# Three edits to an encoder trunk on one core: the order of split products, the queue of a DMA, and blank matmuls at the start

## The chip, the cores and the metric

The kernel runs on one core of one Trainium2 chip. The metric is the time of one execution on the device in microseconds (us); lower is better. Engines are named as in the profile: PE is TensorE's matmul side and PEld its weight loads, DVE is VectorE, ACT is ScalarE, POOL is GpSimd, SP is SyncE, which here only issues DMAs.

## What is computed

A two-layer encoder over 256 tokens of width 2048, all in float32. The reference, cut to its frame:

```python
for i in range(DEPTH):                       # DEPTH = 2
    h = rms_norm(x, norm_mix_g[i])
    if i % 2 == 0:                           # retention heads and 2-D neighbourhood attention
        x = x + retention_na_mixer(h, w_in_ab[j], ..., w_out_ab[j])
    else:                                    # differential attention
        x = x + diff_attention_mixer(h, w_in_c[j], ..., w_out_c[j], i)
    m = rms_norm(mem, norm_mem_g[i])
    x = x + memory_cross_attention(rms_norm(x, norm_xattn_g[i]), m, w_xq[i], w_xkv[i], w_xo[i], ...)
    x = x + swiglu_ffn(rms_norm(x, norm_ffn_g[i]), w_ffn_in[i], w_ffn_out[i])
```

Nearly all of the work is in the products of the 256 token rows with the weight matrices, some 453 MB of weights that are each read once.

## The kernel before, in words

Every weight product runs through `gemm` (line 297). A matrix is cut into column blocks of 512, and a block into units of 256 rows of the matrix (two tiles of 128). A load from HBM (`raw`, 1 MB, three buffers, issued by SP at line 282) holds two units. `prepare` (line 269) makes from half of it the two operands of a unit: ACT rounds the weights to float32r (`wh`, line 292), DVE subtracts to get what is left (`wl`, line 293); each has three buffers. The activations are split in the same way into `hi` and `lo` (tiles named `hTh`/`hTl`, `hTfh`/`hTfl`, `aTh`/`aTl` and so on). A unit is 12 matmuls of 128 x 128 by 512 columns: for each of two token tiles t and each of two weight tiles j, hi times `wh` (line 321), hi times `wl` (322), lo times `wh` (323), all added up in one PSUM tile for each t. `prepare` runs up to three units ahead (`LOOK`).

There are 864 units in 24 products (`plan`, from line 235), in a fixed order. Most products finish one block before the next begins; some begin with two or four blocks interleaved, so that the last rows of the activations may come late. When a block's last unit is done, its `epi` takes the two PSUM tiles away (two blocks' tiles exist), and `Side` (line 30) hands out the other work in small steps, one or two for each unit, each due a number of units after the step before. The framework then orders the instructions of each engine by their priority and by when they should be ready; each engine works through its own queue in order.

`regroup` (line 377) turns a block of 256 x 512 values around without TensorE. DVE transposes 32 x 32 squares (line 389), one DMA of 512 KB writes the squares to HBM (`zd`, line 391, issued by SP), and four DMAs of 128 KB read them back in the other grouping (`zz`, line 394, issued by POOL, each waiting for the write's landing). The reads are handed out two units after the write (`LAND`), and their use three units after that (`MOVE`). `feed` (line 409) uses it for the blocks of the next normalised input: ACT writes hi (line 419), DVE lo (line 421). `act_T` uses it for the FFN's hidden blocks. POOL also computes the powers of `rsqrt_mean` (line 334).

At the start, `feed_first` makes the first input from a transposed copy of x that SP loads in eight parts (`xt`), between the weights. The order of the first units (`start`, line 245) interleaves the first two blocks.

Of the kernel before, what the change touches and what calls it, by code (L numbers as in the profile page):

```python
# [10 lines left out]
F32 = mybir.dt.float32  # L11
# [5 lines left out]
P = 128  # L17
D = 2048
T = 256
# [62 lines left out]
def trunk_kernel(  # L82
# [8 lines left out]
    nc = tc.nc  # L91

    def pool(name, bufs, **kw):
        return ctx.enter_context(tc.tile_pool(name=name, bufs=bufs, **kw))

    const = pool("const", 1)
# [13 lines left out]
    ps_acc = pool("ps_acc", 2, space=bass.MemoryType.PSUM)  # L110
    ps_t = pool("ps_t", 2, space=bass.MemoryType.PSUM)
    ps_a = pool("ps_a", 2, space=bass.MemoryType.PSUM)


    x_sb = const.tile([P, 2, D], F32, name="x_sb")
# [129 lines left out]
    start = [(b, 2 * c + u) for c in range(4) for b in range(2) for u in range(2)]  # L245
    start += [(b, u) for b in range(2, len(cols_ab)) for u in range(8)]
    for layer in range(2):
        j = layer // 2
# [10 lines left out]
        for g0, g1 in FFN_GROUPS:  # L259
            n = 2 * (g1 - g0)  # L260
# [8 lines left out]
    def prepare():  # L269

        i, b, u = units[at["unit"]]
        w2, rows, cols, _ = plan[i]
        c, h = u // 2, u % 2
        if (i, b, c) not in raws:
            raw = raws[i, b, c] = rawp.tile([P, 4, NB], F32, name="raw")
            src = w2[rows[c]:rows[c] + 512, cols[b]:cols[b] + NB].rearrange("(k p) n -> p k n", p=P)
            if at["unit"] == 0:
                nc.sync.dma_start(raw[:, 0:2], src[:, 0:2])
                load_xt(1)
                nc.sync.dma_start(raw[:, 2:4], src[:, 2:4])  # L280
            else:
                nc.sync.dma_start(raw, src)
            for what in OPENING.get(at["unit"], ()):
                (load_xt if what >= 0 else load_x)(what if what >= 0 else -1 - what)
        raw = raws[i, b, c]
        if h:
            del raws[i, b, c]
        wh = hip.tile([P, 2, NB], F32R, name="wh")
        wl = lop.tile([P, 2, NB], F32R, name="wl")
        for j in ((0, 1), (1, 2)) if at["unit"] == 0 else ((0, 2),):  # L290
            js, rs = slice(*j), slice(2 * h + j[0], 2 * h + j[1])
            nc.scalar.copy(wh[:, js], raw[:, rs])  # L292
            nc.vector.tensor_sub(wl[:, js], raw[:, rs], wh[:, js])  # L293
        ahead.append((wh, wl))
        at["unit"] += 1

    def gemm(kts, src, epi, gate=None, steps=1, wide=False):
        hi, lo = src
        w2, rows, cols, order = plan[at["phase"]]
        at["phase"] += 1  # L300
        nu = 2 * len(rows)
        accs, left = {}, {}
        for b, u in order:
            side.drain((gate or {}).get(u, ()))
            if b not in accs:
                pools = ((ps_acc, f"acc{t}") for t in range(2))
                if wide and b in (2, 3):
                    pools = ((ps_t, "pt"), (ps_t, "pt")) if b == 2 else ((ps_a, "pa"), (ps_a, "pa"))
                accs[b] = [q.tile([P, NB], F32, tag=tag, name=f"acc{t}") for t, (q, tag) in enumerate(pools)]
                left[b] = nu  # L310
            while len(ahead) <= LOOK and at["unit"] < len(units):
                prepare()
            wh, wl = ahead.popleft()
            acc = accs[b]
            first, left[b] = left[b] == nu, left[b] - 1
            last = left[b] == 0
            for t in range(2):
                ts = slice(t * P, (t + 1) * P)
                for j in range(2):
                    kt = kts[u // 2] + 2 * (u % 2) + j  # L320
                    nc.tensor.matmul(acc[t], lhsT=hi[:, kt, ts], rhs=wh[:, j], start=first and j == 0, stop=False)  # L321
                    nc.tensor.matmul(acc[t], lhsT=hi[:, kt, ts], rhs=wl[:, j], start=False, stop=False)  # L322
                    nc.tensor.matmul(acc[t], lhsT=lo[:, kt, ts], rhs=wh[:, j], start=False, stop=last and j == 1)  # L323
            if last:
                epi(b, acc)
            side.pump(steps)
# [50 lines left out]
    def regroup(srcs, room=""):  # L377


        if room == "m8":  # L380
            both = m8.tile([P, 2, 4 * T], F32, tag="m8", name="zz")
            zt, zT = both[:, 0], both[:, 1]
        elif room:
            zt, zT = (qk.tile([P, 4 * T], F32, tag=room + x, name="zz") for x in "hl")
        else:
            zt, zT = (vp.tile([P, 4 * T], F32, tag="v" + x, name="zz") for x in "hl")
        zt = zt.rearrange("p (j k t b) -> p j k t b", j=4, k=4, t=2)
        for t in range(2):
            nc.vector.transpose(zt[:, :, :, t], srcs[t].rearrange("p (k j a) -> p j k a", j=4, a=32))
        zd = dram.tile([4, 32, 4, T], F32, name="zd")  # L390
        nc.sync.dma_start(zd.rearrange("i a j n -> (i a) (j n)"), zt.rearrange("p j k t b -> p (j k t b)"))
        yield LAND
        for j in range(4):
            nc.gpsimd.dma_start(zT[32 * j:32 * j + 32].rearrange("a (i n) -> a i n", i=4),  # L394
                                zd[:, :, j].rearrange("i a n -> a i n"))
        yield MOVE - LAND
        return zT.rearrange("p (i k t b) -> p i k t b", i=4, k=4, t=2)
# [11 lines left out]
    def feed(dst, b, srcs, gi, layer, ssr, room):  # L409
        for t in range(2):  # L410
            square_sum(ssr[0][:, t, b:b + 1], srcs[t])
        if b == 3:
            finish_rstd(ssr)
        zT = yield from regroup(srcs, room)
        for k in range(4):
            g = gain(gi, layer, 4 * b + k)
            hi, lo = (x[:, 4 * b + k].rearrange("p (t i b) -> p t i b", t=2, i=4) for x in dst)
            src = zT[:, :, k].rearrange("p i t b -> p t i b")
            nc.scalar.activation(hi, src, AF.Copy, scale=g)
            for t in range(2):  # L420
                nc.vector.scalar_tensor_tensor(out=lo[:, t], in0=src[:, t], scalar=g, in1=hi[:, t].bitcast(F32),
                                               op0=ALU.mult, op1=ALU.subtract)
# [190 lines left out]
    def retention_na(j, hT, rstd, oT, gate):  # L613
# [4 lines left out]
        def epi(b, acc):  # L618
# [26 lines left out]
            else:  # L645
# [9 lines left out]
                tails.append(side.add(gate_T(zs, oT, gi * 4, head_gain(c_ret + j)), 2))  # L655

        gemm(KT4, hT, epi, gate=gate)
        side.drain(tails[:1])
        return {6: tails}
# [46 lines left out]
    def diff_attention(j, hT, rstd, oT, gate):  # L706
        groups = [{} for _ in range(4)]

        def epi(i, acc):
            b, part = i // 3, i % 3  # L710
            g = groups[b]
            if part == 0:
                g["q"], g["tq"] = normed_T(acc, rstd, c_dq + j, "qT")
            elif part == 1:
                g["k"], g["tk"] = normed_T(acc, rstd, c_dk + j, "kT")
                g["tasks"] = [side.add(diff_head(g, hh, 2 * b + hh, j, oT), cond=prepared(g)) for hh in range(2)]
            else:
                g["v"] = tokens(acc, rstd)

        gemm(KT4, hT, epi, gate=gate)  # L720
        for b in range(3):
            side.drain(groups[b]["tasks"])
        return {6: groups[3]["tasks"]}
# [35 lines left out]
    for layer in range(2):  # L759
        j = layer // 2  # L760
        A, B = which
        oT = pair(B, "oT")
        if layer % 2 == 0:
            gate = retention_na(j, hT, ssr[1:], oT, gate)
            kts = (8, 12, 0, 4)
        else:
            nc.vector.scalar_tensor_tensor(out=tabs, in0=tdiff, scalar=-1.0, in1=tdiff, op0=ALU.mult, op1=ALU.max)
            gate = diff_attention(j, hT, ssr[1:], oT, gate)
            kts = KT4
# [21 lines left out]
        mtasks = [side.add(mem_block(b)) for b in range(4)]  # L791

        gemm(kts, oT, lambda b, acc: add_x(acc, b), gate=gate)
        side.drain(mtasks)
        hT = pair(B, "hTx")
# [34 lines left out]
        def act_T(aT, zs, kt):  # L830
            zT = yield from regroup(zs)
            for t in range(2):
                split(*(x[:, kt:kt + 4, t * P:(t + 1) * P].rearrange("p k (i b) -> p k i b", i=4) for x in aT),
                      zT[:, :, :, t].rearrange("p i k b -> p k i b"))

        for g0, g1 in FFN_GROUPS:
            aT = pair(A, "aT")
            n = g1 - g0
# [17 lines left out]
            kts = tuple(4 * b for b in range(n))  # L856
            last = g1 == 11
# [53 lines left out]
```

## Time and profile before

| | us |
|---|---|
| three runs | 2475.91, 2476.86, 2476.88 |
| median | 2476.86 |
| the profiled execution | 2475.84 |
| its span, first to last instruction | 2474.1 |
| PE busy in the span | 2456.3 |

The span is 1.7 us shorter than the time of its own execution. Busy times of PE are modelled from starts, so the distance from one matmul's start to the next is the better measure; it is read from the timeline, where each matmul has its start in the first column.

### The profile page before, as it was taken

What the parts mean: (1) busy time and instruction counts of PE and PEld (TensorE: products, weight loads), DVE (VectorE), ACT (ScalarE), POOL (GpSimd) and SP (SyncE); (2) the same over time, 40 slices, a digit from 0 to 9 for tenths busy, and PEclk for the clock granted to TensorE, in tenths of its full rate; (3) what the DMA queues carried; (4) which work ended last, traced back from release to release, by engine and by line L of the source; (5) the groups of instructions that cost most, each with busy time, mean ns of one, the idle gap of its engine ahead of it and who ended that gap; (6) DMA issues with size and microseconds to landing.
All of it is one profiled execution on the core that took longest, in us unless ns stands there. A gap on an engine that the chain in (4) does not pass through costs nothing.

```text
span 2474.1 us, 28641 instructions
## 1 busy us (share of the span) xinstructions
PE 2456.3 (99%) x11184; PEld 2037.1 (82%) x11184; DVE 1475.7 (60%) x1833; ACT 1187.0 (48%) x1538; POOL 138.2 (6%) x215
## 2 busy tenths in 40 slices
PE   8999999999999999999999999999999999999999
PEld 6888888888888888888888888888888888888887
DVE  6775565675655555555567766767655545555554
ACT  6554464564443444444455555655544444443443
POOL 1000001010000000000010000010100000000000
PEclk9999999999999999999999999999999999999999
DMA  8555567656765666566674555675766656665665
GB/s 288 177 169 179 175 226 245 214 192 213 233 216 200 205 212 225 194 198 226 225 241 164 170 170 168 212 249 171 237 222 210 215 188 214 228 206 200 207 217 175
DMA packets 250184, 511.82 MB, mean 207 GB/s; under 512 B 11328, under 2 KB 11968, under 8 KB 250048
## 3 DMA queue, kind: packets, MB, share of 16 engines
q1 hardware_dynamic: 239568, 484.47, 58.5%
q0 software_dynamic: 8320, 23.08, 4.1%
q10 hardware_dynamic: 2160, 2.44, 0.3%
q8 instruction: 87, 1.43, 0.2%
q14 instruction: 49, 0.40, 0.0%
HBM read 486.88 MB, written 23.07 MB: 206 GB/s over the span
## 4 chain that ended last, share of the span: by engine, by line
PE 92%; DMA 3%; DVE 3%; ACT 1%; POOL 1%; issue 0%; ACTq 0%; SPq 0%; POOLq 0%; DVEq 0%
PE acc L322 30%; PE acc L321 30%; PE acc L323 30%; DMA zz<-zd 2%; DVE wl L293 1%; DMA zd<-zz 1%; PE pt L345 1%; ACT wh L292 0%; PE pt L545 0%; PE pa_s L437 0%; PE pa_s L436 0%; DVE x_sb L741 0%; PE pa_s L435 0%; POOL zz L394 0%; PE pa_r L595 0%
## 5 line engine op out<-in xcount | busy, mean ns | idle before, releaser
L293 DVE TENSOR_TENSOR wl<-raw,wh 128x1024 fp32r<-128x1024 f32 (+1 forms) x865 | 1053.7, 1221 | 870.8 <-ACT wh L292 870.4
L292 ACT CAST wh<-raw 128x1024 fp32r<-128x1024 f32 (+1 forms) x865 | 909.1, 1051 | 1158.2 <-PE acc L323 1132.8
L322 PE MATMUL acc<-wl,hTfh 128*128 128x512 f32 x1408 | 547.9, 389 | 0.6 <-DVE wl L293 0.6
L323 PE MATMUL acc<-wh,hTfl 128*128 128x512 f32 x1408 | 547.7, 389 | 0.0
L321 PE MATMUL acc<-wh,hTfh 128*128 128x512 f32 x1408 | 547.7, 389 | 0.0
L321 PE MATMUL acc<-wh,hTh 128*128 128x512 f32 x832 | 332.0, 399 | 9.8 <-ACT wh L292 8.3
L322 PE MATMUL acc<-wl,hTh 128*128 128x512 f32 x832 | 325.7, 391 | 0.9 <-DVE wl L293 0.9
L323 PE MATMUL acc<-wh,hTl 128*128 128x512 f32 x832 | 325.8, 392 | 0.0
L322 PEld LDWEIGHTS acc<-wl,hTfh 128*128 128x128 f32 x1408 | 264.3, 188 | 56.2 <-DVE wl L293 1.4
L323 PEld LDWEIGHTS acc<-wh,hTfl 128*128 128x128 f32 x1408 | 264.3, 188 | 54.9
L321 PEld LDWEIGHTS acc<-wh,hTfh 128*128 128x128 f32 x1408 | 264.3, 188 | 54.9
L322 PE MATMUL acc<-wl,aTh 128*128 128x512 f32 x704 | 274.0, 389 | 0.2 <-DVE wl L293 0.2
L323 PE MATMUL acc<-wh,aTl 128*128 128x512 f32 x704 | 273.9, 389 | 0.0
L321 PE MATMUL acc<-wh,aTh 128*128 128x512 f32 x704 | 273.9, 389 | 0.0
L321 PEld LDWEIGHTS acc<-wh,hTh 128*128 128x128 f32 x832 | 157.2, 189 | 40.0 <-ACT wh L292 8.3
L323 PEld LDWEIGHTS acc<-wh,hTl 128*128 128x128 f32 x832 | 156.7, 188 | 34.0
L322 PEld LDWEIGHTS acc<-wl,hTh 128*128 128x128 f32 x832 | 157.2, 189 | 31.2 <-DVE wl L293 1.8
L394 POOL DMA_DIRECT2D zz<-zd x160 | 87.3, 552 | 1589.9 <-DMA zd<-zz 1410.9
L322 PEld LDWEIGHTS acc<-wl,aTh 128*128 128x128 f32 x704 | 132.1, 188 | 28.2 <-DVE wl L293 0.8
L321 PEld LDWEIGHTS acc<-wh,aTh 128*128 128x128 f32 x704 | 132.1, 188 | 27.5
L323 PEld LDWEIGHTS acc<-wh,aTl 128*128 128x128 f32 x704 | 132.1, 188 | 27.3
L321 PE MATMUL acc<-wh,oTh 128*128 128x512 f32 x256 | 100.2, 392 | 0.0
(189 smaller groups left out, 1940.3 us busy)
## 6 DMA issues: line engine op xcount, KB each, us to landing
raw<-in_w_ffn_in SPq DMA_DIRECT2D x176, 1024.0 KB, 5.1
raw<-in_w_ffn_out SPq DMA_DIRECT2D x88, 1024.0 KB, 5.1
raw<-in_w_in_ab SPq DMA_DIRECT2D x55, 1024.0 KB, 5.2
raw<-in_w_in_c SPq DMA_DIRECT2D x48, 1024.0 KB, 5.2
zd<-zz SPq DMA_DIRECT2D x40, 512.0 KB, 3.8
zz<-zd POOLq DMA_DIRECT2D x160, 128.0 KB, 5.4
raw<-in_w_out_ab SPq DMA_DIRECT2D x16, 1024.0 KB, 5.1
raw<-in_w_xkv SPq DMA_DIRECT2D x16, 1024.0 KB, 5.0
```

What stands on the lines that cost most here:

```text
L292: nc.scalar.copy(wh[:, js], raw[:, rs])
L293: nc.vector.tensor_sub(wl[:, js], raw[:, rs], wh[:, js])
L321: nc.tensor.matmul(acc[t], lhsT=hi[:, kt, ts], rhs=wh[:, j], start=first and j == 0, stop=False)
L322: nc.tensor.matmul(acc[t], lhsT=hi[:, kt, ts], rhs=wl[:, j], start=False, stop=False)
L323: nc.tensor.matmul(acc[t], lhsT=lo[:, kt, ts], rhs=wh[:, j], start=False, stop=last and j == 1)
L345: nc.tensor.transpose(pt[:, j, t * P:(t + 1) * P], srcs[t][:, c:c + P], ident)
L394: nc.gpsimd.dma_start(zT[32 * j:32 * j + 32].rearrange("a (i n) -> a i n", i=4), zd[:, :, j].rearrange("i a n -> a i n"))
```

## The change

Three edits. Ahead of all other work, DVE clears a tile of 128 x 128 float32, and PE multiplies it by itself 16 times into PSUM tiles that are not read. In a unit, the eight products with `wh` (hi and lo, for both token tiles) come first, and the four with `wl` last. The DMA that writes the squares to HBM is issued by POOL in place of SP.

```diff
@@ -110,6 +110,15 @@
     ps_a = pool("ps_a", 2, space=bass.MemoryType.PSUM)
+    blank = const.tile([P, P], F32, name="blank")
+    nc.vector.memset(blank, 0.0)
+    for _ in range(4):
+        idle = ps_t.tile([P, 2, T], F32, tag="pt", name="idle")
+        for j in range(2):
+            for t in range(2):
+                nc.tensor.matmul(idle[:, j, t * P:(t + 1) * P], lhsT=blank, rhs=blank, start=True, stop=True)
@@ -314,13 +323,17 @@
             last = left[b] == 0
-            for t in range(2):
-                ts = slice(t * P, (t + 1) * P)
-                for j in range(2):
-                    kt = kts[u // 2] + 2 * (u % 2) + j
-                    nc.tensor.matmul(acc[t], lhsT=hi[:, kt, ts], rhs=wh[:, j], start=first and j == 0, stop=False)
-                    nc.tensor.matmul(acc[t], lhsT=hi[:, kt, ts], rhs=wl[:, j], start=False, stop=False)
-                    nc.tensor.matmul(acc[t], lhsT=lo[:, kt, ts], rhs=wh[:, j], start=False, stop=last and j == 1)
+            for low in (False, True):
+                for t in range(2):
+                    ts = slice(t * P, (t + 1) * P)
+                    for j in range(2):
+                        kt = kts[u // 2] + 2 * (u % 2) + j
+                        if low:
+                            nc.tensor.matmul(acc[t], lhsT=hi[:, kt, ts], rhs=wl[:, j], start=False, stop=last and j == 1)
+                            continue
+                        nc.tensor.matmul(acc[t], lhsT=hi[:, kt, ts], rhs=wh[:, j], start=first and j == 0, stop=False)
+                        nc.tensor.matmul(acc[t], lhsT=lo[:, kt, ts], rhs=wh[:, j], start=False, stop=False)
             if last:
@@ -388,7 +401,7 @@
         zd = dram.tile([4, 32, 4, T], F32, name="zd")
-        nc.sync.dma_start(zd.rearrange("i a j n -> (i a) (j n)"), zt.rearrange("p j k t b -> p (j k t b)"))
+        nc.gpsimd.dma_start(zd.rearrange("i a j n -> (i a) (j n)"), zt.rearrange("p j k t b -> p (j k t b)"))
         yield LAND
```

## Rows read from the trace of the kernel before

**Rows 1.** The page: busy us, share of the span and instructions of each engine.
```profile
PE 2456.3 (99%) x11184; PEld 2037.1 (82%) x11184; DVE 1475.7 (60%) x1833; ACT 1187.0 (48%) x1538; POOL 138.2 (6%) x215
```

**Rows 2.** Waits of PE, whole span: us in total, times, longest us.
```profile
PE acc L321 <- ACT wh L292: 8.3, 1, 8.3
PE acc L322 <- DVE wl L293: 2.2, 6, 0.5
PE acc L321 <- DVE z L475: 1.5, 2, 0.8
```

**Rows 3.** Timeline of PE: start us, us, instruction, idle before and releaser.
```profile
8.28 0.80 PE L321 MATMUL acc<-wh,hTh 128*128 128x512 f32 x1 [8.28 <-ACT wh L292]
9.49 0.80 PE L322 MATMUL acc<-wl,hTh 128*128 128x512 f32 x1 [0.42 <-DVE wl L293]
...
13.50 0.63 PE L322 MATMUL acc<-wl,hTh 128*128 128x512 f32 x1
13.92 0.56 PE L323 MATMUL acc<-wh,hTl 128*128 128x512 f32 x1
14.32 0.39 PE L321 MATMUL acc<-wh,hTh 128*128 128x512 f32 x1
...
33.36 0.40 PE L321 MATMUL acc<-wh,hTh 128*128 128x512 f32 x1
...
54.92 0.39 PE L323 MATMUL acc<-wh,hTl 128*128 128x512 f32 x1
56.03 0.47 PE L321 MATMUL acc<-wh,hTh 128*128 128x512 f32 x1 [0.72 <-DVE z L475]
```

**Rows 4.** The chain in order of time: eight float32 matmul records of 128 columns.
```profile
238.91 0.89 PE pa_r L595 x8
```

**Rows 5.** Timeline of ACT between 31 and 51 us.
```profile
31.01 1.05 ACT L292 CAST wh<-raw 128x1024 fp32r<-128x1024 f32 x1 [3.35 <-DMA raw<-in_w_in_ab]
48.61 0.60 ACT L470 ACTIVATE sq<-acc 128x512 f32<-128x512 f32 x1 [0.36 <-PE acc L323]
```

**Rows 6.** Busy time by stretch: PE, PEld, DVE, ACT, POOL, granted clock, DMA share, GB/s.
```profile
8.20:31.00 22.80, 22.31 (x86) 17.92 (x87) 18.47 (x45) 13.39 (x24) 2.82 (x5) 1.00 1.05 333
540.00:565.00 25.00, 24.73 (x109) 20.18 (x108) 19.35 (x37) 14.91 (x27) 7.33 (x13) 1.00 0.97 275
```

**Rows 7.** Timeline of PE at a late low part.
```profile
562.64 0.39 PE L321 MATMUL acc<-wh,hTfh 128*128 128x512 f32 x1
563.30 0.50 PE L322 MATMUL acc<-wl,hTfh 128*128 128x512 f32 x1 [0.27 <-DVE wl L293]
563.64 0.40 PE L323 MATMUL acc<-wh,hTfl 128*128 128x512 f32 x1
```

**Rows 8.** Timeline of ACT around the same place.
```profile
559.34 1.71 ACT L419 ACTIVATE hTfh<-zz,gcol 128x256 fp32r<-128x256 f32 x4 [3.60 <-DMA zz<-zd]
560.95 1.99 ACT L292 CAST wh<-raw 128x1024 fp32r<-128x1024 f32 x2
563.73 1.71 ACT L419 ACTIVATE hTfh<-zz,gcol 128x256 fp32r<-128x256 f32 x4 [0.79 <-DMA zz<-zd]
```

**Rows 9.** Timeline of SP's and POOL's DMA issues there.
```profile
541.06 0.34 SPq L391 DMA_DIRECT2D zd<-zz  x1
545.84 0.34 SPq L391 DMA_DIRECT2D zd<-zz  x1
...
539.98 2.23 POOL L394 DMA_DIRECT2D zz<-zd  x4 [45.03 <-ACT wh L292]
548.46 2.17 POOL L394 DMA_DIRECT2D zz<-zd  x4 [6.26 <-DMA zd<-zz]
550.65 0.75 POOL L334 TENSOR_TENSOR ssxr<-ssxr,mhalf 128x2 f32<-128x2 f32 x1
```

**Rows 10.** The page's DMA issues: KB each, median us to landing.
```profile
zd<-zz SPq DMA_DIRECT2D x40, 512.0 KB, 3.8
zz<-zd POOLq DMA_DIRECT2D x160, 128.0 KB, 5.4
```

## The prediction

> **What bounds the kernel now.** First the page's busy times: PE is busy for 2456.3 of 2474.1 us [rows 1], so the time is the sum of PE's own work and nothing else can give more than some 18 us. That is the frame: 864 units of 12 products are 10368 matmuls, and from 14.32 to 33.36 us seven units, 84 matmuls, take 19.04 us [rows 3], 0.2267 each. A unit is thus 2.72 us. The change leaves the number and the shape of these matmuls as they are, so 10368 x 0.2267 = 2350 us cannot move unless the distance itself does. The second view is PE's waits: 8.3 us for the first weights, 2.2 us in six pieces for a unit's low part, 1.5 us in two pieces for a block's evacuation [rows 2]. The third is PE's timeline at those places, because a wait costs more than the idle time that is booked: at 562.64 the next start comes 0.66 us later and the one behind that 0.34, where two times 0.227 is the rule, so an idle time of 0.27 costs 0.54 [rows 7].
>
> **The blank matmuls.** The first unit runs at half speed: its products stand 0.42 apart at 13.50 and 13.92 [rows 3]. 512 columns in 0.427 us are 1.2 GHz, and 0.2267 is close to 512 columns at 2.4 GHz. The granted clock column says 1.00 for this stretch [rows 6], which doesn't fit those distances; I go by the distances. The first 12 products take 14.32 - 8.28 = 6.04 us, with a wait for the low part among them, against 2.72, so at most 3.3 us are to be had. What the blank work costs: a float32 matmul of 128 columns shows as two records, eight records take 0.89 [rows 4], so 16 matmuls take 32 x 0.111 = 3.6 us at the high clock and 7.1 at the low one. They need only a cleared tile, so I let them start at about 1 us; they end between 4.6 and 8.1, ahead of the first weights at 8.28, and PE has nothing else to do there: cost nothing. Were the weights there at 6, they would cost up to 2 us. If the clock is up by 8.28, the first unit ends 3.3 us sooner at best. What is late next is DMA: its share is 1.05 from 8.2 to 31 us [rows 6], and the ninth unit's load lands when ACT starts to round it, at 31.01, after 3.35 idle; rounding takes 1.05 [rows 5], so this unit can't start before 32.1. Before, it started at 33.36 [rows 3]. So 1.2 us are left of 3.3. Next is the third block at 56.03, where PE waits for DVE to empty a PSUM tile: 1.11 from start to start, 0.88 too much [rows 3]. The chain behind it begins with a square at 48.61 that waits for PE [rows 5], so it moves along with PE and the wait stays. The new order moves it a little: the first token tile's sum is now finished by the tenth product of a unit and not the sixth, 4 x 0.227 = 0.9 us later, the second's still by the twelfth; on the other hand ACT gets a `wh` buffer back after the eighth product, 0.9 sooner. Bounds -0.9 and +0.9; I take 0, since the chain ends with the second tile. **Start: -1.2 us, between -2.1 and 0.**
>
> **Low parts last.** A unit's first `wl` product moves from second to ninth place, 7 x 0.227 = 1.6 us later, while DVE makes it no later. Of the six waits one is in the first unit (0.42, counted above) [rows 3]; the other five have 1.8 us of idle time [rows 2], and with 0.27 more each, as in the one shown [rows 7], they cost 1.8 + 1.35 = 3.1 us. None is longer than 0.5, so 1.6 covers all. The lo times `wh` product moves from third to second place, where it needs the activations' low part 0.23 sooner; at the shown place DVE writes that ahead of the weights' low part, so it is there. Distance between products: the average of 0.2267 holds over neighbours with the same weights (hi, hi) and with others (hi, lo), so I charge nothing for the new neighbours. The `wl` buffer comes back one product later, 0.23 us, three units ahead of need: nothing. At the very end the last block's first token tile comes 0.9 later, of which all but the DVE add of the second tile overlaps: +0.2, between 0 and 0.9. **Together -2.9.**
>
> **Squares by POOL.** SP sheds 40 issues of 0.34 [rows 9]; PE never waited for a load after the first [rows 2], so nothing is gained. POOL gets 40 issues at about 2.17/4 = 0.54 each [rows 9], 22 us on an engine that is 6% busy [rows 1]. The trace has no write of this size from POOL. The nearest rows: SP's 512 KB land after 3.8 us, POOL's reads of 128 KB after 5.4 [rows 10]. So from above +1.6 us a write; from below a gain of 3: the write of 541.06 landed only by about 548 (POOL's wait for it ends at 548.46) [rows 9], at a DMA share of 0.97 [rows 6], and another queue might get it there as fast as the median. I take +1, nearer to POOL's own row.
>
> The Trainium skill ("DMA: Bandwidth & Descriptors", Specifications) gives about 1 us to the first byte for DMAs of GpSimd and 0.6 for those of SP, so by it a write is 0.4 us later; no row here shows that alone, and by it the sum below would be -4.1 and the time 2472.8.
>
> Where does +1 hurt? Not where ACT has room: the blocks of the FFN are 22 of 40 and lie many units apart. It hurts in the stretch from 540 to 565 and its twin in the second layer, where three blocks follow each other. ACT stands 3.60 us for the second block's reads at 559.34; behind it in its queue are two roundings of weights from 560.95, the first done at about 562.0 [rows 8], and PE starts on that unit at 562.64 [rows 7]. So 0.6 us of room: +1 costs 0.4, on ACT and thus ahead of a `wh`, which the late low part doesn't cover. POOL's own queue adds to this: the second write (541.06) now meets POOL at the first block's reads (539.98, 2.23 long) [rows 9], up to 1.1 later. The third block's write (545.84) can end up behind POOL's wait for the second one. I take 0.85 for each layer. **Together +1.7, between 0 and +8.**
>
> **Sum.** -1.2 - 2.9 + 1.7 = -2.4. The profiled execution's 2475.84 becomes 2473.4; the median lies 1.0 above it, and 2476.86 - 2.4 = 2474.5 is forecast.
>
> **The rivals.** (a) All the covers hold: the writes cost nothing, the start gives 2.1, and of the two evacuation waits the one in the second layer shrinks by 0.9 too. -2.1 - 2.9 - 0.9 = -5.9, 2471.0. For it speaks that POOL is nearly idle; against it that ACT already stood still for reads. Chance 0.14.
> (b) Slower: POOL's queue in order. If the third write is queued behind the second block's four reads, it waits from 545.84 to 550.63, behind the power of 0.75 to 551.4 [rows 9]: 5.6 late. The third block's reads are awaited by ACT at 563.73 with 0.79 to go [rows 8]; behind them is the rounding for the unit that starts at 562.64 + 2 x 2.72 = 568.1, ready before at 563.73 + 1.71 + 1.05 = 566.5. Room 1.6, so 4.0 us are lost in each layer, 8.0 in both, and 0.8 at the second write: -4.1 + 8.8 = +4.7, 2481.6, or a little more where DVE's queue stands as well. It decides from 1.6 us of lateness on. Against it: with that write out of the way the second block's reads share DMA with less, and the framework may put the write first. Chance 0.12, of which 0.10 beyond the bound.
> (c) The change doesn't do what it says: the blank work doesn't raise the clock, or it falls again before 8.28 because PE is idle from 4.6 on; then the first unit gains only its wait for the low part, about 0.5, and the queue costs what the order saves: 2476.4. Chance 0.19. For it speaks that the trace shows no work of this kind ahead of a low clock; against it that the clock rose at about 14 after some 6 us of work [rows 3], and the blank work is up to 7.1 long.
>
> **How the numbers follow.** Forecast 0.55, (a) 0.14, (b) 0.12, (c) 0.19. A measurement of this kernel can tell about 0.2%, 5 us, from no change: the bounds are 2471.9 and 2481.8. Faster: (a), 0.14. Slower: the far part of (b), 0.10. Within: 0.76. The range takes in the start's bounds, the tail's and most of the write's, from 2470.8 to 2480.2; (b) and a little of (a) are left out.
>
> **What would show it.** Right: the first product at about 8.3 and the next ones 0.23 apart; the ninth unit at about 32, held by ACT; no wait of PE for `wl`; ACT's wait for `zz` longer by about 1 us around 560 and at its twin, and PE waiting there for `wh`, not `wl`. Wrong: products 0.42 apart after 8.3 (the clock); a third write issued after 550 (rival b); the distance of matmuls in a quiet stretch other than 0.2267, which would move the time by tens of us and break the frame; another order of ACT's and DVE's work, made by the framework, that opens waits where there are none now.

## The result, and the profile after

The changed kernel takes 2487.94 us, median of six runs (2484.94 to 2489.58); six runs of the kernel before beside it have a median of 2476.03 (2473.36 to 2476.88). The ratio is 1.0050, with a 95% interval from 1.0037 to 1.0062: 12 us slower. The profiled execution took 2488.3, its span 2486.4, 12.3 more than before.

The page of the changed kernel, its busy times and its DMA issues, which answer to [rows 1, 10]:

```profile
PE 2467.0 (99%) x11216; PEld 2044.5 (82%) x11216; DVE 1475.9 (59%) x1834; ACT 1189.9 (48%) x1538; POOL 162.2 (7%) x255
...
zd<-zz POOLq DMA_DIRECT2D x40, 512.0 KB, 3.3
zz<-zd POOLq DMA_DIRECT2D x160, 128.0 KB, 5.1
```

PE is busy 10.7 us longer with 32 more records, the blank matmuls. These take 6.4 of it (the first of the stretches below), so other PE work got slower too. The squares land sooner than before, 3.3 us against 3.8. PE's waits of the changed kernel (total, times, longest), which answer to [rows 2]:

```profile
PE acc L335 <- DVE z L488: 5.1, 2, 2.6
PE acc L335 <- ACT wh L301: 2.7, 2, 1.6
PE pt L358 <- DVE z L488: 1.8, 9, 0.2
PE pa_o L448 <- ACT ph L442: 1.4, 1, 1.4
PE idle L121 <- DVE blank L116: 1.1, 1, 1.1
PE pa_o L450 <- DVE vl L523: 1.0, 2, 0.5
PE acc L335 <- ACT xo L442: 0.7, 2, 0.3
...
PE acc L333 <- DVE wl L302: 0.4, 1, 0.4
```

Six waits for `wl` have become one, as the new order wants it. But the wait for `z`, the evacuation of the two first PSUM tile pairs, is 2.5 and 2.6 us in the two layers where it was 0.7 and 0.8, and three kinds of wait are new beside the one for the blank tile: of `pt` for `z`, for `vl` and for `xo`. The table follows the loss along the program. It gives when the first product of a unit starts, from PE's timeline, as the difference to the kernel before in the same place (units counted from 0; kernels other than "after" are the experiments below):

| unit | before, us | after | order_alone | high_held | filled | old_last | by_tile | squares_alone |
|---|---|---|---|---|---|---|---|---|
| 1 | 14.32 | -2.87 | -0.87 | -3.06 | -2.98 | -2.89 | -2.63 | +0.12 |
| 8 | 33.36 | -0.28 | -0.84 | -0.30 | +0.45 | +0.48 | -1.08 | +0.17 |
| 15 | 52.43 | -0.18 | -0.87 | -0.16 | +1.94 | +0.59 | -0.63 | +0.23 |
| 16 | 56.03 | +1.63 | +0.94 | +0.94 | +3.76 | +0.31 | -0.66 | +0.23 |
| 17 | 59.23 | +3.18 | +2.51 | +0.93 | +3.74 | +0.29 | -0.66 | +0.20 |
| 29 | 101.07 | +5.48 | +3.30 | +1.89 | +6.30 | +2.55 | -1.49 | -0.04 |
| 150 | 461.54 | +6.25 | +4.06 | +1.81 | +7.02 | +2.53 | -1.51 | -0.07 |
| 168 | 518.83 | +8.03 | +5.82 | +1.93 | +8.75 | +2.52 | -0.43 | -0.05 |
| 455 | 1304.42 | +5.91 | +3.71 | -0.05 | +6.62 | +1.26 | -2.55 | -1.90 |
| 456 | 1308.11 | +7.72 | +5.52 | +1.04 | +8.43 | +0.59 | -3.00 | -1.90 |
| 457 | 1311.27 | +9.33 | +7.12 | +2.64 | +8.43 | +0.61 | -2.99 | -1.90 |
| 531 | 1542.85 | +11.94 | +9.67 | +2.64 | +10.95 | +0.61 | -2.99 | -1.90 |
| 592 | 1726.28 | +12.91 | +10.62 | +2.59 | +11.90 | -0.19 | -2.73 | -2.69 |
| 611 | 1781.62 | +12.07 | +9.77 | +1.89 | +11.12 | -0.90 | -3.53 | -3.31 |

The column "after" goes up in a few steps. Units 16 and 456, the third block of each layer's first product, start 1.81 later; the units behind them lose another 1.55 and 1.61. From unit 17 to 29 come 2.30, at the attention near 100 us. Units 168 and 592, just behind the two later attentions, and a unit a little ahead of each lose 1.8 together in either layer, and 2.6 us are lost in six steps from unit 457 to 531. Against these stand five gains of 0.5 to 0.8 where the late low parts were.

What the steps at units 16 and 17 are is seen in PE's timeline of the changed kernel, which answers to the last line of [rows 3]:

```profile
57.66 0.77 PE L335 MATMUL acc<-wh,hTh 128*128 128x512 f32 x1 [2.53 <-DVE z L488]
58.23 0.63 PE L336 MATMUL acc<-wh,hTl 128*128 128x512 f32 x1
58.65 0.63 PE L335 MATMUL acc<-wh,hTh 128*128 128x512 f32 x1
59.08 0.63 PE L336 MATMUL acc<-wh,hTl 128*128 128x512 f32 x1
```

PE stands idle for 2.53 us, where it was 0.72, and then the products are 0.42 to 0.43 apart and not 0.227: the slow distance of the start. The stretches of the same kernel, with the columns of [rows 6], say so too: the granted clock is 0.50 behind the first of the two waits, mixed behind the attention near 100 us and behind the second wait, and 1.00 in the others. In the first one it is 1.00 too, though 32 records of 128 columns take 6.38 us there, 0.20 each, where [rows 4] have 0.11: the column doesn't show the slow start.

```profile
1.00:7.50 6.50, 6.38 (x32) 6.18 (x32) 1.25 (x7) 2.39 (x4) 1.80 (x7) 1.00 0.58 176
...
57.60:61.00 3.40, 3.34 (x8) 2.70 (x9) 2.83 (x4) 0.60 (x1) 0.00 (x0) 0.50 0.22 81
61.10:97.00 35.90, 35.90 (x185) 30.18 (x184) 25.71 (x43) 20.51 (x35) 4.13 (x5) 1.00 0.55 161
101.80:105.40 3.60, 3.60 (x11) 2.82 (x11) 3.32 (x6) 0.37 (x1) 0.00 (x0) 0.53 0.84 284
...
1315.80:1320.50 4.70, 4.67 (x15) 3.71 (x16) 3.04 (x5) 1.64 (x2) 0.00 (x0) 0.64 0.12 47
```

Full speed is 2.4 GHz by the distances of [rows 3], so 0.50 is 1.2. The Trainium skill ("TensorE: Matmul & The Clock Gate", "HAM oscillation — how this bites in real kernels") counts half of the time at the low clock as lost; the 3.4 us here give 1.7 as an estimate, and the trace agrees, with 1.55 and 1.61 in the table.

Why `z` comes late is seen on ACT. First the kernel before, its timeline of ACT around 1301 us, in the second layer, where two squares (`sq`, one for each token tile, the first step of the evacuation) stand among the roundings:

```profile
1300.54 0.60 ACT L470 ACTIVATE sq<-acc 128x512 f32<-128x512 f32 x1 [0.30 <-PE acc L323]
1301.90 1.05 ACT L292 CAST wh<-raw 128x1024 fp32r<-128x1024 f32 x1 [0.76 <-PE acc L323]
1302.86 0.59 ACT L470 ACTIVATE sq<-acc 128x512 f32<-128x512 f32 x1
```

Then the changed kernel at the same place, which is 5.91 us later there by unit 455:

```profile
1306.91 1.05 ACT L301 CAST wh<-raw 128x1024 fp32r<-128x1024 f32 x1 [1.67 <-PE acc L336]
1307.86 0.59 ACT L483 ACTIVATE sq<-acc 128x512 f32<-128x512 f32 x1
1309.63 1.05 ACT L301 CAST wh<-raw 128x1024 fp32r<-128x1024 f32 x1 [1.18 <-PE acc L336]
1310.58 0.59 ACT L483 ACTIVATE sq<-acc 128x512 f32<-128x512 f32 x1
```

Before, ACT's order was square, rounding, square; now it is rounding, square, rounding, square. A rounding needs a free `wh` buffer. The last product with `wh` is now the eighth of a unit, not the twelfth, so the buffer comes free before the first token tile's sum is ready, and that rounding has slipped ahead of both squares. The next rounding then stands between the squares, and it waits 1.18 us for the eighth product of the next unit. Behind it, with nothing left to wait for, stands the second square: 1310.58 - 1302.86 = 7.72, of which 5.91 is the shift of the place and 1.81 is new. That is the 1.81 by which unit 456 is late. ACT works through its queue in order here, and this is what the Trainium skill says ("PSUM — Partial Sum Buffer", "Engine vs sequencer instructions": ScalarE's queue is strictly first in, first out).

### The profile page after: what moved, and what is told of

It is laid out like the page before. It is cut to its first block, busy times and chain, and to the rows that moved or that the text cites. A ratio compares the mean times of both kernels' runs of the same rounds, so it can differ in the third digit from the quotient of the medians.

```text
span 2486.4 us, 29138 instructions
## 1 busy us (share of the span) xinstructions
PE 2467.0 (99%) x11216; PEld 2044.5 (82%) x11216; DVE 1475.9 (59%) x1834; ACT 1189.9 (48%) x1538; POOL 162.2 (7%) x255
## 4 chain that ended last, share of the span: by engine, by line
PE 91%; issue 3%; DVE 2%; DMA 2%; POOL 1%; ACT 1%; SPq 0%; DVEq 0%; ACTq 0%; POOLq 0%
PE acc L335 29%; PE acc L336 29%; PE acc L333 29%; DMA raw<-in_w_in_ab 1%; PE pt L358 1%; DVE wl L302 1%; POOL rr L347 1%; ACT wh L301 1%; DVE z L488 0%; PE pa_s L450 0%; PE pa_s L449 0%; PE pa_s L448 0%; DMA zd<-zz 0%; PE pt L558 0%; PE pa_r L608 0%
## 5 line engine op out<-in xcount | busy, mean ns | idle before, releaser
L333 PE MATMUL acc<-wl,hTfh 128*128 128x512 f32 x1408 | 376.3, 389 | 0.0
L333 PE MATMUL acc<-wl,hTh 128*128 128x512 f32 x832 | 224.1, 391 | 0.4 <-DVE wl L302 0.4
L333 PE MATMUL acc<-wl,aTh 128*128 128x512 f32 x704 | 188.1, 389 | 0.0
L404 POOL DMA_DIRECT2D zd<-zz x40 | 22.6, 565 | 1431.3 <-DVE zz L402 1431.3
```

Of the source, the lines that this page charges most:

```text
L404: nc.gpsimd.dma_start(zd.rearrange("i a j n -> (i a) (j n)"), zt.rearrange("p j k t b -> p (j k t b)"))
```

## The experiments

Theory **A**: the new order alone makes the loss, through ACT's queue. The rivals put the loss on another part, or on parts together: **B** on POOL's queue, **C** on the blank matmuls, which shift the start. Within A, A1 says that the `wh` buffer that comes free early is the cause, and A2 that the first token tile's sum, which is ready after the tenth product and not the sixth, makes the chain to `z` long. That the low clock behind the long waits is a cost of its own is a further part of A; *filled* tries it.

**One part at a time.** Each of the three edits alone on the kernel before, and the two others without the order.

*order_alone*: the kernel before with the new loop.

```diff
-            for t in range(2):
-                for j in range(2):
-                    hi x wh, hi x wl, lo x wh
+            for low in (False, True):
+                for t in range(2):
+                    for j in range(2):
+                        hi x wl if low else (hi x wh, lo x wh)
```

> The kernel before with the new order of products alone (no blank matmuls, squares written by SP). Theory A, read from the changed kernel's trace: the order does the harm. It frees a wh buffer after product 8, so ACT's queue has a rounding of weights between the two squares of a block's evacuation that waits for product 8 of the next unit; the third block waits 1.8 us longer in both layers, PE is then idle long enough for its clock to fall, and each fall costs 1.6 us; small waits for transposes follow. So +10 to +13 against before (2486 to 2489), and PE's waits for z about 5 us. Rival B, the squares on POOL's queue, expects within 3 us of before. Rival C, the blank matmuls, expects the same.

Measured: 2488.35 us against 2474.6 for the kernel before, ratio 1.0054 (1.0039 to 1.0069). The whole loss is there without the other two edits. Its waits:

```profile
PE acc L325 <- DVE z L478: 5.1, 2, 2.6
PE pt L348 <- DVE z L478: 1.8, 9, 0.2
...
PE pa_o L440 <- DVE vl L513: 1.0, 2, 0.5
PE acc L325 <- ACT xo L432: 0.7, 2, 0.3
```

They are those of the changed kernel to the tenth, and the time is in the range that A expected. A stands, B and C fall as the cause of the loss. One thing is different: near 102 us this execution has no low clock, though PE waits there as in the changed kernel (1.49 and 0.64 us, against 1.41 and 0.64). So the third of the changed kernel's slow stretches can't be put on the order.

*blank_alone*: the kernel before with the blank matmuls.

```diff
+    blank = const.tile([P, P], F32, name="blank")
+    nc.vector.memset(blank, 0.0)
+    (16 matmuls blank x blank)
```

> The kernel before with the 16 blank matmuls alone. Theory A: the first unit takes 2.9 us instead of 6.0, but the ninth unit is held by the load of its weights at about 33 us, as in the changed kernel (33.08 against 33.36), so 0 to -1 us, 2475 to 2476. Rival C (the blank work or the order of work that the framework makes around it does the harm): +5 or more.

Measured: 2475.51, ratio 1.0004 (0.9995 to 1.0014): nothing, as A expected. In this execution unit 3 starts 0.59 sooner than before, but unit 8 starts 0.63 later, held by a rounding whose input landed late, and then by its low part; the clock falls and unit 12 is 3.38 late. PE's timeline at that place:

```profile
33.98 0.49 PE L330 MATMUL acc<-wh,hTh 128*128 128x512 f32 x1 [0.99 <-ACT wh L301]
35.24 0.50 PE L331 MATMUL acc<-wl,hTh 128*128 128x512 f32 x1 [0.77 <-DVE wl L302]
```

The stretch behind it, with the columns of [rows 6]:

```profile
36.00:39.40 3.40, 3.40 (x9) 2.64 (x8) 2.88 (x5) 2.51 (x6) 0.00 (x0) 0.50 1.04 386
```

A start that is ahead of the loads turns the lead into a wait, and the wait can cost the clock.

*squares_alone*: the kernel before with one word changed.

```diff
-        nc.sync.dma_start(zd.rearrange(...), zt.rearrange(...))
+        nc.gpsimd.dma_start(zd.rearrange(...), zt.rearrange(...))
```

> The kernel before with the DMA of the squares issued by POOL alone. Theory A: writes land in 3.3 us instead of 3.8, PE's five waits for the low part stay within 1 us of their sum of 3.1; -1 to +1 us. Rival B (POOL's queue in order holds the third write of three): +5 to +10, with writes issued after 550 and PE waiting for wh.

Measured: 2472.98, ratio 0.9995 (0.9986 to 1.0004), so no loss. The one profile shows a gain that A had not expected: the five waits for the low part behind the first unit are gone (the steps at units 184, 438, 443, 580 and 608, 3.2 us in all). Its page's DMA issues:

```profile
zd<-zz POOLq DMA_DIRECT2D x40, 512.0 KB, 3.5
```

Its timeline of ACT, at the place of [rows 8]:

```profile
558.52 1.71 ACT L419 ACTIVATE hTfh<-zz,gcol 128x256 fp32r<-128x256 f32 x4
560.13 1.04 ACT L292 CAST wh<-raw 128x1024 fp32r<-128x1024 f32 x1
```

The writes land after 3.5 us, ACT works on the second block's reads at 558.52 without a wait, where it was 559.34 after 3.60 [rows 8], the rounding behind them comes 0.82 sooner, and the late low part of [rows 7] is gone with it. That isn't only a sooner write: POOL issues these reads at 549.93, later than the 548.46 of [rows 9], and they are there sooner all the same. Why they take less time was not settled.

*old_order*: the changed kernel with the loop of before, thus the blank and POOL's writes together.

> The changed kernel with the old order of products, that is the blank matmuls and POOL's writes together. Theory A: all of the loss goes, 2474 to 2476. Rivals B and C: 2480 or more stays.

Measured: 2474.17, ratio 0.9998 (0.9989 to 1.0007), as A expected. No fall of the clock, the `z` waits 1.5 in two as before.

**Why the order costs.** Four kernels, each the changed one with one thing different.

*high_held*: in a block's last unit the eighth product, lo times `wh`, becomes the twelfth, so that the buffer comes free as late as before.

```diff
+            order = [8 products with wh, then 4 with wl]     # in short
+            if last:
+                order.append(order.pop(7))
```

> The changed kernel; in each block's last unit one product of lo with wh (second token tile, second weight tile) is moved behind the products with wl, so that the wh buffer comes free with the twelfth product as in the kernel before, while the first tile's sum is done with the ninth. Theory A1 (the early buffer lets a rounding slip ahead of both squares, and the next rounding then waits between them): the wait of PE for z falls from 2.6 to about 0.8 in both layers, no fall of the clock there, 2476 to 2479. Theory A2 (the late end of the first tile's sum makes the chain long): the wait stays above 2 us, 2484 or more.

Measured: 2479.47 against 2475.7, ratio 1.0015 (1.0005 to 1.0024). One moved product in each block takes away most of the loss. ACT's order is square, rounding, square again, the waits of the transposes are gone, and so are all that was lost between units 457 and 531 and nearly all that was lost at the two later attentions (0.1 at most is left of 1.8 in each; a further 0.7 on the way to unit 592 is a low part that comes late again, in unit 580). But A1 had expected a `z` wait of 0.8 and no fall of the clock, and neither came: the waits are 1.81 and 1.89 us, 1.1 more than before at units 16 and 456, and the clock falls at the second. Timeline of ACT, then DVE, then PE:

```profile
1301.17 0.60 ACT L481 ACTIVATE sq<-acc 128x512 f32<-128x512 f32 x1 [1.89 <-PE acc L332]
1301.85 1.05 ACT L301 CAST wh<-raw 128x1024 fp32r<-128x1024 f32 x1
1302.80 0.59 ACT L481 ACTIVATE sq<-acc 128x512 f32<-128x512 f32 x1
...
1304.08 0.68 DVE L482 TENSOR_REDUCE ss<-sq 128x4 f32<-128x512 f32 x1
1304.75 1.23 DVE L302 TENSOR_TENSOR wl<-raw,wh 128x1024 fp32r<-128x1024 f32 x1
1305.89 0.16 DVE L496 TENSOR_TENSOR ss<-ss,ssxq 128x8 f32<-128x8 f32 x1
...
1309.14 0.47 PE L332 MATMUL acc<-wh,hTh 128*128 128x512 f32 x1 [1.89 <-DVE z L486]
```

DVE at the same place of the kernel before:

```profile
1304.13 0.68 DVE L471 TENSOR_REDUCE ss<-sq 128x4 f32<-128x512 f32 x1
1304.84 0.17 DVE L485 TENSOR_TENSOR ss<-ss,ssxq 128x8 f32<-128x8 f32 x1
```

The second square is where it was before (1302.86), and so is the reduction behind it, so the late first sum (A2) has no part in what stays. Now it is DVE that does a subtraction for `wl` ahead of the small sum `ss`, 1.14 us in the chain to `z`; before, that sum followed at once. The subtraction belongs to a rounding that comes at 1303.66 and not at 1304.62, since the next unit still gives its `wh` buffer back after the eighth product. So it looks like the same kind of cost, on the other engine; no run tries it alone.

*filled*: 11 blank matmuls more ahead of the third block of both layers' first product (extra work, nothing is left out).

```diff
+            if b == 2 and first and at["phase"] in (1, 13):
+                (11 matmuls blank x blank)
```

> The changed kernel with 11 more blank matmuls (22 records, 2.45 us at the full clock) ahead of the third block's first unit in both layers, where PE waits for z. Theory A: the wait is filled with work, so PE's clock doesn't fall, and the products behind stand 0.227 apart and not 0.427; -1.6 in each layer, 2484 to 2485.5. If the clock's fall had nothing to do with PE being idle, or cost nothing: 2488.

Measured: 2486.37, ratio 1.0045 (1.0028 to 1.0062). PE's timeline at the second place:

```profile
1313.77 2.62 PE L330 MATMUL idle<-blank 128*128 128x128 f32 x22
1316.54 0.47 PE L339 MATMUL acc<-wh,hTh 128*128 128x512 f32 x1 [0.16 <-DVE z L492]
1316.85 0.39 PE L340 MATMUL acc<-wh,hTl 128*128 128x512 f32 x1
1317.08 0.39 PE L339 MATMUL acc<-wh,hTh 128*128 128x512 f32 x1
...
```

Three stretches of it, with the columns of [rows 6]:

```profile
33.80:37.20 3.40, 3.40 (x9) 2.72 (x10) 3.40 (x4) 2.67 (x6) 0.00 (x0) 0.55 1.05 387
57.60:61.00 3.40, 3.32 (x24) 2.97 (x24) 2.22 (x5) 0.40 (x2) 1.11 (x1) 1.00 0.79 293
1316.50:1320.50 4.00, 3.96 (x20) 3.33 (x21) 3.15 (x6) 2.17 (x3) 0.64 (x1) 1.00 0.16 57
```

At both places `z` is as late as in the changed kernel (+1.82 and +1.81 in the table), but the clock stays up and the steps behind, 1.55 and 1.61, are -0.02 and 0.00. So the low clock is a cost of its own, 3.2 us for the two, and with the idle time filled it doesn't come. The median is only 1.6 below the changed kernel's, less than the expected 2.4 to 4, and the ranges of the two overlap, so the total alone shows nothing. The profiled execution, at 2487.28 one of the longer of the four, lost elsewhere: the ninth unit's input landed late, PE idled 2.39 us, and the clock fell near 33.8, 1.5 us by unit 15. In `blank_alone` it falls near the same place without the new order, so that fall is put down to the start.

*old_last*: the new order in all units but a block's last one.

```diff
+            order = old if last else new     # in short
```

> The changed kernel with the old order of products in each block's last unit alone, the new order in the other seven eighths. Theory A: ACT's queue has both squares of the third block's wait in a row, ahead of a rounding; the wait for z goes below 0.5 us, no falls of the clock, and the new order's gain at wl stays: 2469 to 2473. If the new order costs something in every unit, most of the 12 us stays: 2484 or more.

Measured: 2473.65, ratio 0.9993 (0.9984 to 1.0003). The median is just above the expected range. The `z` waits are 0.44 at unit 16 and none at 456, so the loss hangs on the last unit of each block and not on the new order in all others. The table ends at -0.90, since a longer wait and a fall of the clock near 98 us take some 2 back.

*by_tile*: the low parts last within each token tile, so that the first tile's sum is ready at the sixth product as before, and `wh` comes free at the tenth.

```diff
+            for t in range(2):
+                for low in (False, True):
```

> The changed kernel with the wl products last within each token tile and not within the unit: the first tile's sum is done with the sixth product as before, a wh buffer comes free after the tenth. Theory A: ACT's queue is square, rounding, square as in the kernel before, the wait for z is 0.6 to 0.9, no falls of the clock; a wl product is first needed at the fifth place, 0.7 us later than before, which covers most waits for it: 2471 to 2474.

Measured: 2473.64, ratio 0.9993 (0.9983 to 1.0002). Square, rounding, square on ACT, no fall of the clock, the `z` waits 0.68 and 0.35. Units 168 and 592 still lose 1.1 each behind a wait for `vl` and one for `xo`; that part comes with this order too. At unit 592 ACT's rounding at 1719.68 stands between the two `vh` (1718.77 and 1720.64); before, it came behind both (1722.55, 1723.91, then 1724.49).

**Is there a version that beats both?** Three kernels without the blank matmuls, with more executions: *squares_more* (the same as squares_alone), *old_last_squares* and *by_tile_squares* (its order and POOL's writes).

> The squares' writes on POOL's queue and nothing else, again with more executions. If the waits for the low parts (2.2 us idle, some 3 us with what hangs on them) went because SP's loads no longer stand behind the writes, 2.5 to 3.5 us less than the kernel before: ratio 0.9986 to 0.9990. If that was an accident of one profile, ratio 0.9996 to 1.0004.

> The kernel before with the squares' writes on POOL's queue, and the low parts last in every unit but a block's last one, no blank matmuls. If the two evacuation waits shrink as they did with the blank matmuls in front (0.72 and 0.80 to 0.44 and 0), 1 us less than with the squares alone: ratio 0.9982 to 0.9988. If the order brings nothing once the low parts are no longer late, the same as with the squares alone.

> The kernel before with the squares' writes on POOL's queue, and the low parts last within each token tile in all units, no blank matmuls. The evacuation waits shrink by 0.4 us each, but the waits at the end of attention (0.3 for the value's low part and 0.3 for the product behind it, 1.1 us from start to start in each layer) come with this order: 1.4 us more than with the squares alone, ratio 0.9988 to 0.9996. If those waits came from the blank matmuls' shift alone, ratio 0.9982 to 0.9988.

Measured against 2476.41: 2473.15, ratio 0.9989 (0.9980 to 0.9997); 2472.59, ratio 0.9985 (0.9977 to 0.9994); 2473.11, ratio 0.9987 (0.9978 to 0.9996). All three are 3 to 4 us faster than the kernel before beside them; the first measurement of the same edit, `squares_alone`, gave 1 to 2 us and no clear difference. They can't be told from each other, so that an order brings anything beside POOL's writes is not shown. The ratio of by_tile_squares lies in the range for waits that come from the blank matmuls, but its trace has the losses of 1.1 at units 168 and 592 without them: those come with the order.

## Why the prediction was wrong

The forecast was 2474.5 and no measurable change; 2487.94 is above the range. Point by point:

**The step that failed** is in the first part: "it moves along with PE and the wait stays ... on the other hand ACT gets a `wh` buffer back after the eighth product, 0.9 sooner. Bounds -0.9 and +0.9; I take 0, since the chain ends with the second tile." The early buffer was seen and booked as a gain. It is where the loss starts: it lets one rounding go ahead of the squares, and the next one then waits between them for a unit that isn't done. The wait grew by 1.81 in each layer, twice the upper bound, 3.6 us in all. `high_held`, which puts ACT's order back, takes 0.72 of each away; the 1.09 that stay are the subtraction that DVE now does ahead of `ss`, which the trace shows and no run tries alone. With the old order in the last units (`old_last`), all of it goes. That the framework might make another order of ACT's and DVE's work stands in the prediction's last part as what would prove it wrong, but it had no chance and no price.

**A price that was missing**: the low clock behind an idle PE. The trace of before shows an idle 0.72 at unit 16 and 1.58 near 97 us and no low clock after the start, so the text priced a longer wait at its own length only. The falls cost 1.55, 1.61 and, near 102 us, 1.58: 4.7 us. `filled` shows this for the first two. The third is there in this execution, but not in `order_alone`, and `old_last` has one near 98 us, so it isn't shown to be the order's.

**Waits that had no term**: the transposes (2.6 us between units 457 and 531) and the two later attentions (1.8 each) wait now too. `high_held` gives back all of the first and nearly all of the second, so they hang on the same early buffer. At unit 475 ACT's queue is rounding, square, rounding, square once more: the second rounding waits 1.24 us until 1372.88, and the second square comes at 1373.83, 1.9 later than before beyond the shift of the place. At unit 592 a rounding stands ahead of both `vh`, where it came behind both before, and DVE does its `wl` at 1735.70, ahead of `vl` at 1736.84. Timeline of ACT in the changed kernel:

```profile
1734.61 1.06 ACT L301 CAST wh<-raw 128x1024 fp32r<-128x1024 f32 x1 [1.25 <-PE acc L336]
1735.57 1.25 ACT L522 ACTIVATE vh<-acc,ssmr 128x512 fp32r<-128x512 f32 x2
```

**Low parts last, -3.1**: right as a term. The five places (the steps at units 184, 438, 443, 580 and 608) give -0.57, -0.53, -0.80, -0.79 and -0.60 in the changed kernel, 3.3 together. But `squares_alone` gets 3.2 at the same places without the order. Two edits that mend the same waits don't add up, and the sum had them as if the queue could only spoil what the order gains.

**Squares by POOL, +1.7**: the wrong sign. The bound below nothing was named and the value was put near POOL's small reads. The write took 3.3 us in the changed kernel and 3.5 in `squares_alone`. The mechanism of rival (b) is there: in `squares_alone` POOL issues the third write at 549.35 and not 545.84, behind its power, and the reads behind it 2.7 later. Its price is not: ACT starts on them at 564.00, 0.27 later than in [rows 8], and PE doesn't wait. The Trainium skill's page quoted in the prediction also gives a fit for such transfers ("DMA: Bandwidth & Descriptors", "Anatomy of one DMA — SWDGE (gpsimd) path": 2.0 us and the bytes by 436 GB/s), by which 512 KB take 3.2 as an estimate. The medians of POOL's writes lie at that or above, 3.2 to 3.8 in ten kernels. Whether POOL's writes land later than SP's, as the prediction drew from the Trainium skill's figures for the first byte, is not shown: SP's took 3.8 and 3.9 with the old order (before, `blank_alone`), but 2.8 in `order_alone`, 0.5 sooner than POOL's in the changed kernel.

**Start, -1.2**: right in its first half. The first product came at 8.52, the next ones 0.23 apart, and unit 1 was 2.87 sooner. PE's timeline of the changed kernel, which answers to [rows 3], then ACT's, which answers to [rows 5]:

```profile
8.52 0.50 PE L335 MATMUL acc<-wh,hTh 128*128 128x512 f32 x1 [1.08 <-ACT wh L301]
8.86 0.39 PE L336 MATMUL acc<-wh,hTl 128*128 128x512 f32 x1
...
33.08 0.50 PE L335 MATMUL acc<-wh,hTh 128*128 128x512 f32 x1 [1.61 <-ACT wh L301]
```

```profile
31.98 2.00 ACT L301 CAST wh<-raw 128x1024 fp32r<-128x1024 f32 x2 [5.25 <-DMA raw<-in_w_in_ab]
```

The first of these two fences is PE's, the second ACT's. The ninth unit is held by the load as predicted, but that rounding began at 31.98 and not at 31.01, so -0.28 is left. In the seven kernels with the blank matmuls it began between 31.18 and 32.89, in the six without them between 30.71 and 31.57. The load is no fixed point: it came later in most kernels that ran ahead of it. Why was not settled.

Together, from the column "after": the longer `z` waits 3.6, the falls of the clock 4.7, transposes 3.4 with the smaller steps up to unit 150, attentions 3.5, the attention near 100 us another 0.7, low parts -3.8 with the small steps beside them, start -0.2, tail 0.3. That is 12.2 of 12.3; the rest is rounding.

## What to carry to other kernels

When a buffer is freed sooner, look at which engine refills it and what else is in that engine's queue: the refill can be put ahead of work that the critical path needs, and the next refill then waits in the middle of it. Price an idle stretch of TensorE at its length and, where a change makes it grow, allow for a slow stretch behind it too (1.6 us for each here). Before two gains are added, see whether both mend the same wait.

## What the runs showed of the hardware that was not expected

Falls of the clock didn't follow the length of one idle stretch. Idle times of 2.53 and 2.62 us in the changed kernel, and 1.89 at 1309 us in `high_held`, had a stretch at 0.50 behind them; 1.72 and 1.81 in `high_held` had none, but neither had 2.32 at 33.8 us in `old_last`, 2.54 near 99 us in `high_held` and 2.64 near 98 us in `old_last_squares`. Two short ones close together, 0.99 and 0.77 in `blank_alone`, had one; 1.41 and 0.64 near 101 us had one in the changed kernel, and 1.49 and 0.64 at the same place in `order_alone` had none. So a fall near such a wait differs from kernel to kernel, and it can be shown only in the trace at hand. And 512 KB writes from POOL's queue landed in 3.2 to 3.8 us (medians of 40 in ten kernels), those from SP's in 2.8, 3.8 and 3.9 (three kernels): no queue is the faster one in all.
